# Where the block sums of a seven-product phase are made: four instructions per unit on VectorE or on GpSimd

## The chip, the cores and the metric

The kernel runs on one core of one Trainium2 chip. The metric is the device time of one launch in microseconds (us); smaller is better. Three runs of the kernel before took 1160.32, 1160.54 and 1163.41 us, median 1160.54.

## The reference

One layer of a diffusion backbone over 512 latent and 256 context tokens with 1024 channels. The part that matters here is the second feed-forward block, which works on the 512 latent tokens alone:

```python
def swiglu(h, w1, w3, w2):
    return (jax.nn.silu(h @ w1) * (h @ w3)) @ w2

def ffn_sublayer(h_in, shift, scale, gate, norm_w, w1, w3, w2):
    h = modulate(rms_norm(h_in, norm_w), shift, scale)
    return h_in + 0.5 * gate * swiglu(h, w1, w3, w2)
...
x = ffn_sublayer(x, mx[6], mx[7], mx[8], norm3_w, ffn2_w1, ffn2_w3, ffn2_w2)
```

The inner width is 2816, which is 22 slices of 128. One slice, with its 128 columns of `w1` and of `w3`, is called a unit below.

## The kernel before

**Split products.** Every float32 matrix product is made of three products. Each operand is split into a high part (`oph`, rounded by ScalarE's copy) and a low part (`opl`, the remainder, a subtraction on VectorE), and `mm3` adds high x high, low x high and high x low. So each 128x512 piece of weights costs one ScalarE cast of 128x512 and, behind it, one VectorE subtraction of 128x512 (`Stream.operand`, `Stream.split`, L138 to L147).

**Seven products in place of eight.** Units 4 to 21 of this block (class `Winograd`, made at L1692, run at L1728) multiply a 2x2 grid of weight blocks by a 2x2 grid of token blocks with seven block products. On the weight side a unit's four blocks q0 to q3, which arrive together in one 1 MB load (tile `block`, 128x2048), give seven operands: q0, s = q2+q3, q1, q0' = s-q0, q2' = q0-q2, q3 and q1' = q1-q0'. The four sums are the subject of the change. They overwrite the block in place, except s, which has a tile of its own. In the kernel before, GpSimd makes them, apart from unit 4, whose sums VectorE makes.

**Order on TensorE.** A unit runs T1, B21, T2, T3, then B11 of the next unit, then T4 and B22 of its own (method `unit`, L750): seven products of 12 matmuls of 256 columns. Two of them, T4 and B22, add to PSUM banks that T3 and T1 filled. VectorE has to read those banks first (`ev_u3`: u3 = W+u2, then u3 = Z+u3, with W the bank of T3 and Z the bank of T1).

**Slots.** `Flow.slot` (L105) is called ahead of each product. It writes out, in this order, the first part of the evacuation of the product before, then one more operand from the list, then the rest of the evacuation. At most five operands (`OPS`) are alive, so an operand is written out about four products ahead of its use. In slot order VectorE's part of a unit is: u2 and operand s of the next unit; the two adds of u3 and operand q1; operand q0'; W+u2 and W*silu, operand q2', the low part gl of the result; Z+u2, operand q0 of the unit after, Z*u3 and gl; operand q3; operand q1'.

**What sets the order.** The whole phase stands under `nc.ordered = "all"` (L1727): every instruction of VectorE, ScalarE, GpSimd and TensorE keeps the order in which it is written (`Pinned`, L60, is why nearly all rows of the profile carry the line L60). Each engine works off its queue in that order.

**Between the units.** After units 4, 8, 12, 16 and 18 a part of the down projection runs (`down_flow`, L638), with four slices each, two after unit 18: eight column blocks of 12 (6) matmuls of 512 columns, one operand of `w2` (from tiles `raw`) for each 4 matrix tiles, and one update of `x` by VectorE per column block. The last part (units 18 to 21) is written without pinned order, and a scheduler placed its first column blocks ahead of T4 of unit 21.

Of the kernel before, what the change touches and what calls it, by code (L numbers as in the profile page):

```python
# [173 lines left out]
def layer_kernel(ctx: ExitStack, tc: tile.TileContext, xT, wfirst, wst, wada, wuq, wkpe, cols, wrope, vnw, rope, out):  # L174
    nc = Core(tc)
# [6 lines left out]
    st = Stream(nc, raws, opp, OPS, wst)  # L182
# [81 lines left out]
    u0, rw0 = st.raw_pool.tile([P, 2048], F32, tag="block", bufs=BLOCKS, name="block_first"), st.raw()  # L264
# [137 lines left out]
    class SsqAcc:  # L402
        def __init__(self, pool, n, eng):
            self.pool, self.n, self.eng = pool, n, eng
            self.acc = None
            self.squares = []
# [259 lines left out]
    U_UP2 = U_IN + 22  # L666
# [11 lines left out]
    class Winograd:  # L678


        def __init__(self, pool, n, u0, blocks, g_tile, sl_bufs):
            self.sl_bufs = sl_bufs
            self.ready = (None,)
            self.pool, self.n, self.u0, self.blocks, self.g_tile = pool, n, u0, blocks, g_tile

# [10 lines left out]
        def wants(self, f):  # L696
            q, s1, eng = [], [], []

            def first():
                if self.ready[0] != f:  # L700
                    self.prep(f)
                q[:], s1[:], eng[:] = self.ready[1], [self.ready[2]], [self.ready[3]]
                a = st.operand(q[0])
                eng[0].tensor_sub(q[2], q[0], q[2])
                eng[0].tensor_sub(q[0], s1[0], q[0])
                return a

            def third():
                a = st.operand(q[1])
                eng[0].tensor_sub(q[1], q[1], q[0])  # L710
                return a

            of = lambda i: lambda: st.operand(q[i])
            return first, lambda: st.operand(s1[0]), third, of(0), of(2), of(3), of(1)

        def plan(self, flow, f0, downs, late=False):
# [132 lines left out]
    blocks = {"B11": hb(0, 0), "B21": hb(4, 0), "B22": hb(4, 384), "T1": hb(0, 384)}  # L849
# [65 lines left out]
    wino = Winograd(gp, 384, U_UP1, blocks, g_tile, 1)  # L915
# [698 lines left out]
    f2 = f2ctx.enter_context(tc.tile_pool(name="ffn2", bufs=2))  # L1614
# [74 lines left out]
    evac(0, 1)  # L1689
    diffs(3)  # L1690
    blocks = {"B11": B11, "B21": B21, "B22": B22, "T1": T1, "T2": T2, "T3": T3, "T4": T4}
    wino = Winograd(f2, 256, U_UP2, blocks, g2_tile, 2)  # L1692
    wino.prep(NPLAIN2, nc.vector)
    flow = Flow(OPS)
    wino.plan(flow, NPLAIN2, lambda f: [(CHUNKS2[ci], U_DN2 + starts2[ci]) for ci in ends2(f)])
# [141 lines left out]
```

## Time and profile before

| What | Value |
|---|---|
| Median of three runs | 1160.54 us |
| Span of the profiled execution | 1160.9 us |
| TensorE busy | 1139.5 us, 98% |
| VectorE busy | 906.1 us, 78% |
| ScalarE busy | 532.0 us, 46% |
| GpSimd busy | 320.9 us, 28% |
| Mean granted TensorE clock | 0.999 |
| The changed phase (units 4 to 21) | about 850 to 1141 us of the span |

A row of the timeline reads: start in us, duration in us, engine, line, operation, tile written <- tiles read, shapes, how many were merged; in brackets how long the engine sat idle before it and what ended that. Buffer numbers are left out of names, and `u2`, `u3`, `p1` and `s1` appear as `u`, `u`, `p` and `s`. A chain row reads: start, duration, engine, tile and line. A group row reads: line, engine, operation, tiles, shapes, count, then busy time, mean ns of one and idle time before them. VectorE's rows overlap a little: a 128x512 subtraction is listed with 0.68 us, and an independent instruction behind it starts 0.60 us after it did. One profiled execution gives all these rows.

### The profile page before, as it was taken

The numbers are of one execution on the slowest core, as the hardware profiler recorded it, in microseconds if no ns is written. First come the engines' busy times: TensorE is split into PE (matmuls) and PEld (weight loads), VectorE is DVE, ScalarE is ACT, GpSimd is POOL, SyncE is SP. The second block draws the span as 40 slices with busy tenths as digits, with TensorE's granted clock in tenths as the row PEclk, the third lists the DMA queues.
The fourth block names the chain that finished last, engine by engine and source line by source line (L and its number), as shares of the span: only waits on it lengthen the run. The fifth ranks groups of instructions, "written<-read, shape, count | busy, mean of one in ns | idle before, by whom it ended". The sixth has DMA issues, their size and how long they took to land. (4 is left out here: it accounts for less than half of the span.)

```text
span 1160.9 us, 18702 instructions
## 1 busy us (share of the span) xinstructions
PE 1139.5 (98%) x7070; PEld 1071.9 (92%) x7070; DVE 906.1 (78%) x1668; ACT 532.0 (46%) x1075; POOL 320.9 (28%) x279
## 2 busy tenths in 40 slices
PE   9999999999999999999999999999999999999998
PEld 5699999999999999999988788999999989898997
DVE  4778799889888779866746969869876959686884
ACT  4455431441244213444745549876543535353441
POOL 0011401320333013300017637670013325142330
PEclk9999999999999999999999999999999999999999
DMA  9441244334334664412242111002221322333312
GB/s 351 146 140 37 91 145 137 119 127 164 110 127 145 210 209 158 144 57 82 82 144 90 57 37 55 19 1 76 72 92 55 132 87 74 109 110 109 110 37 91
DMA packets 34650, 125.89 MB, mean 108 GB/s; under 512 B 3584, under 2 KB 10496, under 8 KB 29056
## 3 DMA queue, kind: packets, MB, share of 16 engines
q1 hardware_dynamic: 34416, 124.63, 31.3%
q8 instruction: 56, 0.92, 0.3%
q14 instruction: 34, 0.28, 0.1%
q10 hardware_dynamic: 144, 0.06, 0.0%
HBM read 122.58 MB, written 2.10 MB: 107 GB/s over the span
## 5 line engine op out<-in xcount | busy, mean ns | idle before, releaser
L60 DVE TENSOR_TENSOR opl<-block,oph 128x512 fp32r<-128x512 f32 x216 | 190.6, 888 | 35.5 <-ACT oph L60 33.4
L60 POOL TENSOR_TENSOR block<-block 128x512 f32<-128x512 f32 x70 | 103.7, 1481 | 393.5 <-DVE opl L60 390.8
L60 ACT CAST oph<-block 128x512 fp32r<-128x512 f32 x216 | 134.0, 621 | 144.6 <-PE mm L60 91.7
L60 PE MATMUL mm<-gh,oph 128*128 128x384 f32 (+1 forms) x440 | 155.2, 353 | 0.0
L60 PE MATMUL mm<-gl,oph 128*128 128x384 f32 (+1 forms) x440 | 154.9, 352 | 0.0
L60 PE MATMUL mm<-gh,opl 128*128 128x384 f32 (+1 forms) x440 | 154.9, 352 | 0.0
L60 DVE SCALAR_TENSOR_TENSOR x<-mm,g,x 128x256 f32<-128x256 f32 (+2 forms) x184 | 83.0, 490 | 49.9 <-PE mm L60 49.3
L60 ACT CAST oph<-raw 128x512 fp32r<-128x512 f32 x106 | 64.4, 619 | 93.8 <-PE mm L60 68.0
L60 PEld LDWEIGHTS mm<-gh,opl 128*128 128x128 f32 x440 | 82.6, 188 | 5.7
L60 PEld LDWEIGHTS mm<-gh,oph 128*128 128x128 f32 x440 | 82.6, 188 | 5.6
L60 PEld LDWEIGHTS mm<-gl,oph 128*128 128x128 f32 x440 | 82.6, 188 | 5.5
L60 DVE TENSOR_TENSOR opl<-raw,oph 128x512 fp32r<-128x512 f32 x106 | 73.2, 704 | 9.5 <-ACT oph L60 9.0
L60 POOL TENSOR_TENSOR s<-block 128x512 f32<-128x512 f32 x35 | 52.3, 1495 | 101.8 <-DVE gl L60 73.3
L60 POOL TENSOR_TENSOR block<-s,block 128x512 f32<-128x512 f32 x35 | 47.5, 1357 | 77.0 <-DVE opl L60 76.6
L60 PE MATMUL mm<-hl,oph 128*128 128x384 f32 x192 | 64.6, 336 | 1.8 <-DVE hl L60 1.8
L60 PE MATMUL mm<-hh,oph 128*128 128x384 f32 x192 | 64.5, 336 | 0.0
L60 PE MATMUL mm<-hh,opl 128*128 128x384 f32 x192 | 64.3, 335 | 0.0
L60 DVE SCALAR_TENSOR_TENSOR junk<-raw,cb 128x1024 bf16<-128x1024 f32 x48 | 60.3, 1263 | 0.1
L60 PE MATMUL one<-hh,oph 128*128 128x384 f32 x144 | 48.7, 338 | 0.0
L60 PE MATMUL one<-hl,oph 128*128 128x384 f32 x144 | 48.7, 338 | 0.0
L60 PE MATMUL one<-hh,opl 128*128 128x384 f32 x144 | 48.6, 337 | 0.0
L60 DVE SCALAR_TENSOR_TENSOR raw<-raw,cb 128x1024 f32<-128x1024 f32 x32 | 41.0, 1289 | 7.7 <-DMA raw<-wada 7.4
(649 smaller groups left out, 3461.6 us busy)
## 6 DMA issues: line engine op xcount, KB each, us to landing
raw<-wst SPq DMA_DIRECT2D x77, 512.0 KB, 3.7
block<-wst SPq DMA_DIRECT2D x36, 1024.0 KB, 4.9
raw<-wada SPq DMA_DIRECT2D x56, 512.0 KB, 4.0
block<-wada SPq DMA_DIRECT2D x7, 1024.0 KB, 7.4
x<-xT SPq DMA_DIRECT2D x6, 512.0 KB, 6.7
raw<-wfirst SPq DMA_DIRECT2D x8, 256.0 KB, 6.4
out<-x SPq DMA_DIRECT2D x7, 256.0 KB, 2.2
block_first<-wada SPq DMA_DIRECT2D x2, 512.0 KB, 8.0
```

The costliest lines, as they stand in the source:

```text
L60: return lambda *a, **k: self.tc.keep_in_program_order(f(*a, **k))
```

## The change

For this phase alone (`on_vector=True`) the four sums of each unit from 5 on are made by VectorE, each in the slot of an operand. The TensorE, ScalarE and DMA instructions stay the same, and so does the list of operands. Unit 4 keeps VectorE and gets the new places too. The first feed-forward block's seven-product phase keeps GpSimd.

```diff
-        def __init__(self, pool, n, u0, blocks, g_tile, sl_bufs):
-            self.sl_bufs = sl_bufs
+        def __init__(self, pool, n, u0, blocks, g_tile, sl_bufs, on_vector=False):
+            self.sl_bufs, self.on_vector = sl_bufs, on_vector
...
             of = lambda i: lambda: st.operand(q[i])
+            v = nc.vector
+
+            def first_v():
+                if self.ready[0] == f:
+                    q[:], s1[:] = self.ready[1], [self.ready[2]]
+                else:
+                    r = st.block(wst, (self.u0 + 2 * f) // 2)
+                    q[:] = [r[:, i * 512 : i * 512 + 512] for i in range(4)]
+                return st.operand(q[0])
+
+            def sum_v():
+                if not s1:
+                    s1.append(self.tmp("s1", 512, 2))
+                    v.tensor_add(s1[0], q[2], q[3])
+                return st.operand(s1[0])
+
+            def third_v():
+                v.tensor_sub(q[2], q[0], q[2])
+                return st.operand(q[1])
+
+            def second_v():
+                v.tensor_sub(q[0], s1[0], q[0])
+                return st.operand(q[0])
+
+            def fourth_v():
+                v.tensor_sub(q[1], q[1], q[0])
+                return st.operand(q[1])
+
+            if self.on_vector:
+                return first_v, sum_v, third_v, second_v, of(2), of(3), fourth_v
             return first, lambda: st.operand(s1[0]), third, of(0), of(2), of(3), of(1)
...
-    wino = Winograd(f2, 256, U_UP2, blocks, g2_tile, 2)
+    wino = Winograd(f2, 256, U_UP2, blocks, g2_tile, 2, True)
```

`nc.vector` is the pinned engine here, so a sum stands in VectorE's queue directly ahead of the low-part subtraction of the operand with which it is written. `st.operand` first writes ScalarE's cast of the operand, then VectorE's subtraction that reads both.

## The prediction

> **What bounds the kernel now.** I read the page first, for the engine that is never idle, then the chain of waits for this phase, then the timelines of VectorE, TensorE, GpSimd and ScalarE over one unit.
>
> ```profile
> span 1160.9 us, 18702 instructions
> PE 1139.5 (98%) x7070; PEld 1071.9 (92%) x7070; DVE 906.1 (78%) x1668; ACT 532.0 (46%) x1075; POOL 320.9 (28%) x279
> ```
>
> TensorE sets the time. The chain of waits runs over it:
>
> ```profile
> 894.87 5.76 PE mm L60 x48
> 900.63 1.44 PE one L60 x12
> 902.07 2.91 PE mm L60 x24
> ```
>
> These rows give a unit's length: four products 5.76, the next unit's B11 1.44, T4 and B22 2.88, together 10.08 us, with no gap between products. The gaps that there are stand ahead of T4:
>
> ```profile
> 911.89 0.28 PE L60 MATMUL mm<-b11h,opl 128*128 128x256 f32 x1
> 913.19 0.36 PE L60 MATMUL one<-t4h,oph 128*128 128x256 f32 x1 [1.02 <-ACT oph L60]
> ...
> 923.68 0.36 PE L60 MATMUL mm<-t4h,oph 128*128 128x256 f32 x1 [0.19 <-DVE u L60]
> ```
>
> ```profile
> L60 PE MATMUL mm<-t4h,oph 128*128 128x256 f32 x36 | 10.7, 298 | 0.6 <-DVE u L60 0.4
> L60 PE MATMUL one<-t4h,oph 128*128 128x256 f32 x36 | 10.4, 289 | 2.3 <-ACT oph L60 2.1 <-DVE u L60 0.2
> ```
>
> The last two rows are groups over the time from unit 4 on and hold T4's matmuls of high parts, the first of each product among them: 2.9 us idle. Matmuls follow each other every 0.12 us, though one is listed with 0.28, so counted from start to start a gap is 0.16 longer (911.89 to 913.19 is 1.30, less 0.12: 1.18). Eight such gaps make 2.9 + 8 x 0.16 = 4.2 us. That is all that this phase can give back.
>
> Why T4 waits is seen on VectorE, here from one u3 to the next:
>
> ```profile
> 901.30 0.88 DVE L60 TENSOR_TENSOR u<-mm,u 128x256 f32<-128x256 f32 x2
> 902.09 0.68 DVE L60 TENSOR_TENSOR opl<-block,oph 128x512 fp32r<-128x512 f32 x1
> 903.03 1.73 DVE L60 TENSOR_TENSOR opl<-block,oph 128x512 fp32r<-128x512 f32 x1 [0.25 <-ACT oph L60]
> 904.68 0.42 DVE L60 TENSOR_TENSOR mm<-mm,u 128x256 f32<-128x256 f32 x1
> 905.14 0.43 DVE L60 TENSOR_TENSOR mm<-mm,sl 128x256 f32<-128x256 f32 x1
> 905.48 1.80 DVE L60 TENSOR_TENSOR opl<-block,oph 128x512 fp32r<-128x512 f32 x1
> 907.21 0.41 DVE L60 TENSOR_TENSOR gl<-mm,gh 128x256 fp32r<-128x256 f32 x1
> 907.54 0.42 DVE L60 TENSOR_TENSOR mm<-mm,u 128x256 f32<-128x256 f32 x1
> 907.87 1.12 DVE L60 TENSOR_TENSOR opl<-block,oph 128x512 fp32r<-128x512 f32 x1
> 908.92 0.42 DVE L60 TENSOR_TENSOR mm<-mm,u 128x256 f32<-128x256 f32 x1
> 909.77 0.43 DVE L60 TENSOR_TENSOR gl<-mm,gh 128x256 fp32r<-128x256 f32 x1 [0.44 <-ACT gh L60]
> 910.30 1.49 DVE L60 TENSOR_TENSOR opl<-block,oph 128x512 fp32r<-128x512 f32 x2
> 911.70 0.42 DVE L60 TENSOR_TENSOR u<-one,p 128x256 f32<-128x256 f32 x1
> 912.03 0.68 DVE L60 TENSOR_TENSOR opl<-s,oph 128x512 fp32r<-128x512 f32 x1
> 912.63 0.88 DVE L60 TENSOR_TENSOR u<-one,u 128x256 f32<-128x256 f32 x2
> ```
>
> This cycle takes 912.63 - 901.30 = 11.33 us, longer than TensorE's 10.08. The first add of u3 ends at 912.63 + 0.42 = 913.05 and T4, which adds to the bank it reads, starts at 913.19: 0.14 later. (The profile names a cast, but that cast's tile was long split; the gap at 923.68 names `u`.) So T4 starts 0.14 us after u3's first add, and where VectorE's cycle exceeds 10.08 us the difference appears ahead of T4.
>
> **The change part by part.**
>
> *Removed: GpSimd's sums, and with them VectorE's slow subtractions.*
>
> ```profile
> 905.44 1.30 POOL L60 TENSOR_TENSOR s<-block 128x512 f32<-128x512 f32 x1 [1.23 <-DMA block<-wst]
> ```
>
> ```profile
> L60 DVE TENSOR_TENSOR opl<-block,oph 128x512 fp32r<-128x512 f32 x98 | 92.7, 953 | 13.3 <-ACT oph L60 11.5
> L60 DVE TENSOR_TENSOR opl<-raw,oph 128x512 fp32r<-128x512 f32 x28 | 18.9, 681 | 0.1
> L60 DVE TENSOR_TENSOR opl<-s,oph 128x512 fp32r<-128x512 f32 x16 | 11.0, 685 | 0.3
> ```
>
> The same subtraction means 0.95 us from `block` and 0.68 from `raw` or `s`. The slow ones run beside a GpSimd sum: that of 905.48 starts 0.04 after GpSimd's of 905.44 and lasts 1.80. With all seven at 0.60 spacing the cycle is: u3 0.80, operands q1 and q0' 1.20, W twice 0.80, operand 0.60, gl and Z+u2 0.66, operand 0.60, Z*u3 to gl 0.85 (908.92 to 909.77), gl to the next operand 0.53, that and q1' 1.20, u2 0.33, operand s 0.60: 8.2 us. So the removal returns 11.3 - 8.2 = 3.1 us of VectorE a unit.
>
> The Trainium skill ("SBUF — State Buffer", section "SBUF: two separate sides") says that VectorE and GpSimd share a port pair under an exclusive lock, and that the loser blocks for the whole instruction. By it the subtraction of 905.48 would wait to 906.74 and end near 907.4; the row ends at 907.28, so the trace agrees. By that rule too the sum has seven fast subtractions.
>
> *Added: four sums a unit.* VectorE makes such a sum in 0.69 us when GpSimd is quiet (unit 4 has one):
>
> ```profile
> 850.15 0.69 DVE L60 TENSOR_TENSOR block<-block 128x512 f32<-128x512 f32 x1
> ```
>
> Four at 0.60 spacing: +2.4 us, cycle 10.6.
>
> *Added: a wait behind three of them.* Where GpSimd made the sum, the cast of s, q0' or q1' could run while VectorE did other things. Now VectorE's queue holds sum, then the subtraction of that very operand, which needs ScalarE's cast, which needs the sum. Nothing may pass: u3, and T4 behind it, queue there. The price by rows:
>
> ```profile
> 909.37 0.37 ACT L60 CAST gh<-mm 128x256 fp32r<-128x256 f32 x1 [1.01 <-DVE mm L60]
> 909.64 0.63 ACT L60 CAST oph<-block 128x512 fp32r<-128x512 f32 x1
> ```
>
> VectorE's row of 908.92 ends at 909.34, ScalarE's cast starts at 909.37 and ends at 909.74, VectorE goes on at 909.77: 0.03 each way, and a 128x512 cast is 0.63. From a sum's start to the subtraction's start: 0.69 + 0.03 + 0.63 + 0.03 = 1.39 in place of 0.60, +0.79 each, three times: +2.4. q2' escapes, since q1's and q0's operands lie between its sum and its use. Bounds: nothing (casts somehow early), cycle 10.6; or the waits in full with the subtractions still at 0.95, 13.0 + 7 x 0.27 = 14.9. I take 13.0 (8.2 + 2.4 + 2.4): the fast rows are those without GpSimd beside them, and GpSimd has nothing left here.
>
> *From the cycle to the time.* Per unit T4 is late by 13.0 - 10.08 = 2.9 us more, wherever a full cycle lies between two T4s:
> - 7 full cycles (to units 6, 7, 10, 11, 14, 15, 20): 7 x 2.9 = 20.3.
> - 4 cycles to a unit ahead of a down part (8, 12, 16, 18): s gives way to a `raw` operand without a sum, so 1.39 less, 11.6: 4 x 1.5 = 6.0.
> - 6 first units (4, 5, 9, 13, 17, 19), where VectorE has caught up:
>
> ```profile
> 884.63 0.28 PE L60 MATMUL one<-t1h,oph 128*128 128x256 f32 x1
> ```
>
> ```profile
> 886.15 0.62 ACT L60 CAST oph<-block 128x512 fp32r<-128x512 f32 x1 [0.92 <-PE one L60]
> ```
>
> Unit 5: the cast of q3 waits for T1's end, 886.15, so q3's subtraction starts at 886.80, the sum q1' at 887.40, its subtraction at 888.79, u2 at 889.39, the sum s at 889.72, its subtraction at 891.11, u3 at 891.71, ending at 892.13; T4 can go at 892.27 where 884.63 + 5 x 1.44 = 891.83 was due: 0.45, say 0.5 each: 3.0. (If u2 alone waited, 0.1.)
> - The end: TensorE fills the time ahead of unit 21's T4 with the last down part:
>
> ```profile
> 1138.51 0.43 DVE L60 TENSOR_TENSOR one<-one,u 128x256 f32<-128x256 f32 x1 [3.96 <-PE one L60]
> ```
>
> VectorE waits 3.96 us there, so that T4 costs nothing; the filler's first `raw` subtraction comes behind unit 20's late queue, about 0.8.
>
> Inside the down parts I cost the sums at nothing: a column block lasts 2.72 us (next rows), and update 0.67, sum to subtraction 1.39 and subtraction 0.60 make 2.66. That cover is nearly used up.
>
> ```profile
> 876.67 0.75 DVE L60 SCALAR_TENSOR_TENSOR x<-mm,g,x 128x512 f32<-128x512 f32 x1 [1.37 <-PE mm L60]
> ...
> 879.39 0.75 DVE L60 SCALAR_TENSOR_TENSOR x<-mm,g,x 128x512 f32<-128x512 f32 x1 [1.37 <-PE mm L60]
> ```
>
> ```profile
> block<-wst SPq DMA_DIRECT2D x36, 1024.0 KB, 4.9
> ```
>
> The block loads neither move nor multiply. A buffer comes free with the subtraction of q1'; the first cast from its new load is due 9.0 us of VectorE's queue later (0.60, u2 0.33, s 1.99, u3 0.80, q2' and q1 1.20, q0' 1.99, W 0.80, operand 0.60, gl and Z+u2 0.66), and landing takes 4.9, so I cost it at nothing too.
>
> Sum: 20.3 + 6.0 + 3.0 + 0.8 = 30.1 us of gaps in place of 4.2: +25.9, so 1160.9 + 25.9 = 1186.8 for the span; the median run stands 0.4 below the profiled one: 1186.4.
>
> **The rivals.**
> - *Only throughput counts.* If the casts did not hold VectorE, the cycle would be 10.6. A first unit would then leave some 0.6 us of slack ahead of T4, and a full cycle uses 0.5 of it: about 1.5 us of gaps in all, 1158 us, and 1156.3 with none. For it: 3.1 us of contention go and only 2.4 come. Against it: the queue's written order. It decides from a cycle below about 11.0, where gaps would again sum to some 4 us. The Trainium skill ("GPSIMD Engine Reference", section "Engine selection") recommends VectorE for elementwise work on a tile, GpSimd being about twice as slow for two inputs; the rows (0.69 against 1.30) agree, and this rival is what that rule would give. Chance 0.08.
> - *The waits are shorter or partly covered.* With one full wait of three the cycle is 11.4, with two 12.2: at 11.8 the full cycles cost 7 x 1.7 and the others some 3: 1160.5 + 15 - 4.2 = 1171. For it: the second subtraction of 910.30 shows no wait for its cast. Against: that cast hung on no VectorE sum just ahead. Chance 0.11.
> - *More than the sum.* Subtractions stay at 0.95, or VectorE is still late when a down part or a load needs it: at 14.9, 7 x 4.8 + 4 x 3.4 + 4 = 51, so 1160.5 + 51 - 4.2 = 1207. For it: the thin cover of 0.06 us. Against: the `raw` and `s` rows. Chance 0.07.
> - *The change does not do what it says:* sums that move away from their operands. The phase's order is pinned; 0.01, time unchanged.
>
> **How the numbers follow.** My forecast has 0.73; its time is 1186.5, its own range 1180 to 1193 (a tenth of a us on the cycle is worth 1.1 us over eleven cycles; I allow 0.6). The range to record reaches into the second and third rivals: 1172 to 1198. About 0.3% (3.5 us) can be told from no change. Faster: half of the first rival, 0.04. Same: the rest of it and the last, 0.05. Slower: 0.91.
>
> **What would show it.** VectorE's u3 to u3 cycle of a middle unit near 13.0 us; three idle stretches of about 0.7 us on VectorE a unit, ended by the cast, ahead of subtractions from `s` and `block`; subtractions from `block` near 0.69; gaps near 2.9 us ahead of T4 in units 6, 7, 10, 11, 14, 15, 20 and near 1.5 in 8, 12, 16, 18; down parts without gaps; GpSimd idle after 846 us. A cycle under 11 us, or sums whose subtractions follow after 0.60, would prove me wrong.

## The result, and the profile after

The changed kernel takes 1192.6 us (median of 5 runs, 1191.6 to 1194.8), the kernel before 1160.5 (5 runs, 1159.7 to 1163.4). The ratio is 1.0268, with a 95% interval of 1.0254 to 1.0283: 32.1 us slower, where 26.0 were forecast. Five runs more of the changed kernel, beside twenty of the kernel before, gave 1.0262 (1.0248 to 1.0276).

First the page of the changed kernel: the span, then each engine's busy time and share.

```profile
span 1189.7 us, 18651 instructions
PE 1144.9 (96%) x7070; PEld 1074.9 (90%) x7070; DVE 918.0 (77%) x1736; ACT 531.6 (45%) x1075; POOL 225.7 (19%) x211
```

GpSimd has 68 instructions fewer and VectorE 68 more (17 units of four sums). VectorE is busy only 11.9 us longer, and still the span grows by 28.8: most of what was added is not work, it is waiting. Where that shows is in TensorE's groups of T4's high-part matmuls (count, then busy time, mean ns, and idle time ahead with what ended it):

```profile
L60 PE MATMUL mm<-t4h,oph 128*128 128x256 f32 x36 | 11.6, 323 | 16.6 <-DVE u L60 11.2 <-ACT oph L60 5.4
L60 PE MATMUL one<-t4h,oph 128*128 128x256 f32 x36 | 10.8, 299 | 8.4 <-DVE u L60 6.5 <-ACT p L60 1.9
```

2.9 us of idle time ahead of T4 have become 25.0. TensorE's timeline has it unit by unit; these are the first matmuls of T4 of units 5, 6, 7 and 8:

```profile
893.49 0.35 PE L60 MATMUL one<-t4h,oph 128*128 128x256 f32 x1 [0.47 <-ACT p L60]
...
906.59 0.36 PE L60 MATMUL mm<-t4h,oph 128*128 128x256 f32 x1 [2.80 <-DVE u L60]
...
919.70 0.36 PE L60 MATMUL one<-t4h,oph 128*128 128x256 f32 x1 [2.81 <-DVE u L60]
...
931.35 0.36 PE L60 MATMUL mm<-t4h,oph 128*128 128x256 f32 x1 [1.35 <-ACT oph L60]
```

From T4 to T4 it is 13.10 and 13.11 us in full cycles and 11.65 ahead of a down part, against 10.08 of TensorE's own work. VectorE's timeline over the same unit, from one u3 to the next, has the reason:

```profile
906.03 0.88 DVE L60 TENSOR_TENSOR u<-mm,u 128x256 f32<-128x256 f32 x2
906.82 0.68 DVE L60 TENSOR_TENSOR block<-block 128x512 f32<-128x512 f32 x1
907.42 0.68 DVE L60 TENSOR_TENSOR opl<-block,oph 128x512 fp32r<-128x512 f32 x1
908.02 0.68 DVE L60 TENSOR_TENSOR block<-s,block 128x512 f32<-128x512 f32 x1
909.45 0.69 DVE L60 TENSOR_TENSOR opl<-block,oph 128x512 fp32r<-128x512 f32 x1 [0.74 <-ACT oph L60]
...
914.71 0.69 DVE L60 TENSOR_TENSOR block<-block 128x512 f32<-128x512 f32 x1
916.14 0.69 DVE L60 TENSOR_TENSOR opl<-block,oph 128x512 fp32r<-128x512 f32 x1 [0.74 <-ACT oph L60]
...
917.08 0.68 DVE L60 TENSOR_TENSOR s<-block 128x512 f32<-128x512 f32 x1
918.53 0.69 DVE L60 TENSOR_TENSOR opl<-s,oph 128x512 fp32r<-128x512 f32 x1 [0.76 <-ACT oph L60]
919.13 0.88 DVE L60 TENSOR_TENSOR u<-one,u 128x256 f32<-128x256 f32 x2
```

The cycle is 919.13 - 906.03 = 13.10 us. Three times a sum is followed by 0.74 or 0.76 us of nothing and then by the subtraction of what it summed (908.02 to 909.45, 914.71 to 916.14, 917.08 to 918.53). The sum q2' at 906.82 has no such wait: its subtraction comes two operands later. The chain of waits walks the same loop; here is the wait behind 908.02, one row for each link (start, duration, engine, tile):

```profile
908.02 0.69 DVE block L60
908.80 0.63 ACT oph L60
909.45 0.69 DVE opl L60
```

From the sum's end to the cast 0.09 us, the cast 0.63, 0.02 back. In the groups of VectorE the subtractions from `block` have become as fast as the others, 0.687 in place of 0.953, and the waits stand ahead of these and of those from `s`:

```profile
L60 DVE TENSOR_TENSOR opl<-block,oph 128x512 fp32r<-128x512 f32 x98 | 67.2, 687 | 28.3 <-ACT oph L60 27.3
L60 DVE TENSOR_TENSOR opl<-s,oph 128x512 fp32r<-128x512 f32 x16 | 11.1, 691 | 12.2 <-ACT oph L60 12.2
```

### The profile page after: what moved, and what is told of

Its sections match the earlier page's. It is cut to its first block, busy times and chain, and to the rows that moved or that the text cites. A ratio compares the mean times of both kernels' runs of the same rounds, so it can differ in the third digit from the quotient of the medians.

```text
span 1189.7 us, 18651 instructions
## 1 busy us (share of the span) xinstructions
PE 1144.9 (96%) x7070; PEld 1074.9 (90%) x7070; DVE 918.0 (77%) x1736; ACT 531.6 (45%) x1075; POOL 225.7 (19%) x211
## 5 line engine op out<-in xcount | busy, mean ns | idle before, releaser
L60 DVE TENSOR_TENSOR opl<-block,oph 128x512 fp32r<-128x512 f32 x216 | 164.2, 763 | 50.1 <-ACT oph L60 48.7
L60 POOL TENSOR_TENSOR block<-block 128x512 f32<-128x512 f32 x36 | 53.2, 1478 | 250.1 <-DVE opl L60 248.7
L60 ACT CAST oph<-s 128x512 fp32r<-128x512 f32 x36 | 22.3, 620 | 64.5 <-DVE s L60 29.1
L60 POOL TENSOR_TENSOR s<-block 128x512 f32<-128x512 f32 x18 | 29.8, 1657 | 91.1 <-DVE gl L60 73.2
```

Of the source, the lines that this page charges most:

```text
L60: return lambda *a, **k: self.tc.keep_in_program_order(f(*a, **k))
```

## The experiments

The open question was not whether VectorE waits, but whether these waits are the whole loss. Rivals: the sums' own time on VectorE, the new places of the sums, or TensorE's granted clock, which falls in the changed kernel (below). Where a kernel below keeps the sums on VectorE, it changes where in the queue they stand. All ratios are to the kernel before on the same chip.

**No sum directly ahead of its cast.** All four sums stay on VectorE, each behind some operand that was loaded or summed earlier, so that its own operand comes a slot or more later:

```diff
-                return st.operand(q[0])
+                a = st.operand(q[0])
+                self.early = q, s1
+                if s1:
+                    early()
+                else:
                     s1.append(self.tmp("s1", 512, 2))
                     v.tensor_add(s1[0], q[2], q[3])
...
+                return a
...
+            def q3_v():
+                a = st.operand(q[3])
+                early()
+                return a
...
-                return first_v, sum_v, third_v, second_v, of(2), of(3), fourth_v
+                return first_v, lambda: st.operand(s1[0]), of(1), of(0), q2_v, q3_v, of(1)
```

`early` makes q2' and q0' of the next unit; `q2_v` writes operand q2' and then the sum q1'.

> All 68 sums stay on VectorE, but each is made one or more slots ahead of the operand that reads it: s in the slot of q0, q2' and q0' in the slot of the q3 before, q1' in the slot of q2'. Theory (a cast's wait behind a sum holds VectorE's queue): the u3-to-u3 cycle falls from 13.1 to about 10.6 us, the gaps ahead of T4 from 29.5 us to at most 3, and the time to 1158 us (1156 to 1161). Rival (four more VectorE instructions a unit are what costs, wherever they stand): the cycle stays near 13 us and the time within 3 us of 1192.

Measured: 1169.5 us, ratio 1.0066 (1.0052 to 1.0080). With the same 68 sums on the same engine, 2.0 of the 2.7 per cent are gone. But 1158 was not reached. VectorE's timeline of this kernel:

```profile
903.39 0.88 DVE L60 TENSOR_TENSOR u<-mm,u 128x256 f32<-128x256 f32 x2
...
905.66 0.43 DVE L60 TENSOR_TENSOR mm<-mm,u 128x256 f32<-128x256 f32 x1 [0.20 <-PE mm L60]
...
911.53 0.69 DVE L60 TENSOR_TENSOR block<-block 128x512 f32<-128x512 f32 x1
912.25 0.69 DVE L60 TENSOR_TENSOR block<-s,block 128x512 f32<-128x512 f32 x1
...
914.39 0.87 DVE L60 TENSOR_TENSOR u<-one,u 128x256 f32<-128x256 f32 x2
```

The cycle is 11.00 us, not 10.6. Two small pieces explain most of it: the add of W waits 0.20 for TensorE (this is T4's own lateness coming round: u3 releases T4, T4's end releases W), and a sum that reads the result of the sum ahead of it starts 0.72 after it, not 0.60. What that makes ahead of T4 stands in the view of T4's tile (idle us, times):

```profile
  DVE u L60: 8.1, 11
```

Eleven gaps, 8.1 + 11 x 0.16 = 9.9 us, about 0.9 behind every full cycle and every cycle ahead of a down part. At a cycle of 11.0 the prediction's first rival had some 4 us of gaps, since it gave each first unit 0.6 us of slack; there is none, the second unit already waits in full. T4's gaps are 5.7 us more than the 4.2 of before, the time 7.8 us more; in the profiled runs 0.9 us of the rest lie ahead of this phase, and what else there is stays open.

**One wait less, one wait more.** In the first of these kernels s is summed a slot earlier, behind operand q0; two waits are left. In the second q0' goes to a tile of its own, and q2' is summed directly ahead of its own cast; that makes four.

```diff
-                return st.operand(q[0])
-
-            def sum_v():
+                a = st.operand(q[0])
                 if not s1:
                     s1.append(self.tmp("s1", 512, 2))
                     v.tensor_add(s1[0], q[2], q[3])
+                return a
+
+            def sum_v():
                 return st.operand(s1[0])
```

```diff
-                v.tensor_sub(q[2], q[0], q[2])
...
-                v.tensor_sub(q[0], s1[0], q[0])
+                q0 = q[0]
+                q[0] = self.tmp("d0", 512, 2)
+                v.tensor_sub(q[0], s1[0], q0)
+                s1[0] = q0
...
+            def q2_v():
+                v.tensor_sub(q[2], s1[0], q[2])
+                return st.operand(q[2])
...
-                return first_v, sum_v, third_v, second_v, of(2), of(3), fourth_v
+                return first_v, sum_v, third_v, second_v, q2_v, of(3), fourth_v
```

> As the changed kernel, but s alone is made early, in the slot of q0; q0' and q1' still stand directly ahead of their operands. Theory: one wait of 0.79 us less in a full cycle, 12.3 us in place of 13.1 (7 x 0.8 = 5.5 us less), the first units lose their gap of 0.6 (3 us less), and the cycles ahead of a down part take in the s of the next unit (4 x 0.6 = 2.4 us more): about 6 us less, 1186 us. Rival (the load of the sums): 1192 us, cycle 13.1.

> As the changed kernel, but the fourth sum, q2', is moved directly ahead of its operand too (q0' goes to a tile of its own so that q0 lives on). The count of VectorE instructions is the same. Theory: one more wait of 0.79 us in every cycle, full ones 13.9 us and those ahead of a down part 12.4: 11 x 0.8 = 8.7 us more than the changed kernel, about 1201 us. Rival (the load of the sums): 1192 us as before.

Measured: 1183.3 us with two, ratio 1.0183 (1.0166 to 1.0200); 1211.7 with four, ratio 1.0429 (1.0408 to 1.0451), and 1208.9, ratio 1.0410 (1.0388 to 1.0433), when it ran again. T4 of units 6 and 7 with two waits, then of units 5, 6 and 7 with four:

```profile
905.37 0.36 PE L60 MATMUL mm<-t4h,oph 128*128 128x256 f32 x1 [1.35 <-DVE u L60]
...
917.62 0.35 PE L60 MATMUL one<-t4h,oph 128*128 128x256 f32 x1 [1.94 <-DVE u L60]
```

```profile
897.76 0.36 PE L60 MATMUL one<-t4h,oph 128*128 128x256 f32 x1 [0.47 <-ACT p L60]
...
911.71 0.36 PE L60 MATMUL mm<-t4h,oph 128*128 128x256 f32 x1 [3.65 <-DVE u L60]
...
925.67 0.35 PE L60 MATMUL one<-t4h,oph 128*128 128x256 f32 x1 [2.16 <-DVE u L60]
```

The cycle is 12.25, 13.10 and 13.95 us for two, three and four waits: 0.85 us each, evenly. From none to two it was 1.25, since the kernel with none has the small idle pieces named above. Whether it is s or q2' that is added makes no difference to the cycle; the number of waits does. The time does not grow as evenly: 9.3 us from two to three (1183.3 to 1192.6), then 16 to 19. With two waits the cycle is as expected and the time 2.7 us under the expected 1186: in the second unit behind a down part T4 waits 1.35 us (unit 6) and not the 1.94 of the next (unit 7), 0.6 less in each of units 6, 10, 14 and 20. With four the cycle is as expected and the time 8 to 11 us over the expected 1201. What else four waits cost is taken up below.

**The same places on GpSimd.** The changed kernel's order with the sums back on GpSimd: `v = nc.vector if self.ready[0] == f else nc.gpsimd`.

> The places of the changed kernel in the written order, but units 5 to 21 make the four sums on GpSimd. Theory (VectorE's own queue is what waits): GpSimd's queue runs ahead of VectorE's as it did, so the time is that of the kernel before, 1160 us within 3, with subtractions from block at a mean near 0.95 us. Rival (spreading the sums over four slots is what costs, on whichever engine): above 1180 us.

Measured: 1164.3 us, beside 1161.8 for the kernel before, ratio 1.0017 (1.0006 to 1.0028). The group of subtractions:

```profile
L60 DVE TENSOR_TENSOR opl<-block,oph 128x512 fp32r<-128x512 f32 x98 | 91.7, 942 | 13.1 <-ACT oph L60 11.4
```

Their idle time is 13.1 as before the change (13.3), and they are slow again. So it is not the spreading over four slots that costs; the same order with another engine as summer has no such waits. Most of the 2 us above the kernel before is unit 4, whose sums VectorE still makes in the new places: its B21 waits 0.70 us there and its T4 0.34.

**No sums at all.** This is an edit of the kernel before: the sums of units 5 to 21 are left out, and the operands are split from the blocks as they were loaded; all else runs.

```diff
+            def bare():
+                r = st.block(wst, (self.u0 + 2 * f) // 2)
+                q[:] = [r[:, i * 512 : i * 512 + 512] for i in range(4)]
+                return st.operand(q[0])
+
             of = lambda i: lambda: st.operand(q[i])
+            if self.bare and self.ready[0] != f:
+                return bare, of(2), of(1), of(0), of(2), of(3), of(1)
```

> The kernel before without the four sums of units 5 to 21: the seven operands are split from the blocks as they were loaded, so their count, casts and subtractions stay, and the products are of other operands. Theory (GpSimd's sums slow VectorE's subtractions, nothing else makes the gaps): subtractions from block at 0.69 us in this phase, no gap ahead of T4 above 0.2 us, 3 to 4 us under the kernel before, 1157 us. Rival (the subtractions from block are slow of themselves): mean near 0.95 us, gaps and time as before.

Measured: 1159.3 us, ratio 0.9972 (0.9963 to 0.9981), and no gap ahead of T4. The difference is the 3 to 4 us that were expected; 1157 was expected from 1160.5, and beside it here the kernel before took 1162.7.

```profile
L60 DVE TENSOR_TENSOR opl<-block,oph 128x512 fp32r<-128x512 f32 x114 | 78.4, 687 | 25.6 <-ACT oph L60 23.9
```

(The idle time in this row holds up nobody: T4 never waits.) Without GpSimd's sums beside it the subtraction takes 0.687 us, so these were what slowed it to 0.953. The Trainium skill ("SBUF — State Buffer", section "SBUF: two separate sides") gives the exclusive lock that the prediction drew on as the mechanism; this run agrees with it. And 3.4 us (1162.7 to 1159.3) is all that the sums cost in the kernel before.

**TensorE kept busy.** In the changed kernel the granted clock means 0.990 to 0.996 over its runs, in the kernel before 0.997 to 1.000. To see whether this costs time, 20 matmuls that nobody reads were put into the idle time ahead of T4 in the seven units after a full cycle:

```diff
+                if f in warm:
+                    w = self.blocks["T4"][0]
+                    for i in range(20):
+                        nc.tensor.matmul(nxt[0][1][:, 256:512], w[:, 0, :128], w[:, 0, :], start=True, stop=True, skip_group_check=True)
```

> The changed kernel with 20 more matmuls of 256 columns (2.4 us), whose results nobody reads, behind B11 in units 6, 7, 10, 11, 14, 15 and 20, where TensorE stood idle 2.9 us. Theory A (the idle stretches lower the granted clock, and that costs time of its own): the clock stays at 1.00 and the time falls by 1 to 3 us against the changed kernel on the same chip. Theory B (VectorE's cycle hides the slower matmuls): the clock stays at 1.00 and the time is the same within 1 us. Neither changes the spacing of T4, 13.1 us in middle units.

The changed kernel ran beside it once more:

> The changed kernel as it is, beside the others on the same chip: 1.027 times the kernel before, clock between 0.990 and 0.996, with slower runs where the mean clock is lower.

Measured: 1193.0 us, ratio 1.0264 (1.0250 to 1.0278), beside 1192.7 and 1.0262 without the matmuls. The clock stood at 0.999 to 1.000. T4 of unit 6 now waits 0.41 us behind the extra matmuls in place of 2.80, and starts no earlier in its cycle:

```profile
905.13 2.56 PE L60 MATMUL one<-t4h 128*128 128x256 f32 x20
...
908.10 0.35 PE L60 MATMUL mm<-t4h,oph 128*128 128x256 f32 x1 [0.41 <-DVE u L60]
```

The lower clock costs the changed kernel nothing that can be measured: VectorE sets the pace there, and TensorE's slower matmuls use up idle time that it would have had in the next unit. In the profiled run of the changed kernel T4 of unit 10 ran slowly (shown at the end); the idle time ahead of T4 of unit 11 is 1.52 us for that, in place of 2.81 in unit 7, and from T4 to T4 it is 13.10 us all the same.

The same with four waits, 28 such matmuls ahead of a full cycle's T4 and 16 ahead of a down part, beside the kernel with four waits again:

> e5_four_waits with extra matmuls whose results nobody reads behind B11: 28 (3.4 us) in units 6, 7, 10, 11, 14, 15, 20 and 16 (1.9 us) in 8, 12, 16, 18. T4 to T4 stays 13.9 us in middle units. Theory A (in e5 the clock fell in units ahead of a down part, where TensorE and not VectorE sets the time, so slower matmuls cost in full): the clock rises from 0.983 to above 0.995 and the time falls towards the 1201 us that the waits alone give, at least 5 us below e5. Theory B (the slower matmuls are hidden in e5 as they are in the changed kernel): the clock rises, the time stays within 2 us of e5.

> e5_four_waits as it is, beside it on the same chip: 1.043 times the kernel before, clock near 0.984.

Measured: 1206.3 us, ratio 1.0374 (1.0359 to 1.0389), against 1.0410 (1.0388 to 1.0433) without: 2.6 us less, at a clock of 0.997 to 0.999 in place of 0.983 to 0.987. The intervals just touch, and the gain lies between the two theories, the 5 us of A and the 2 us of B. The traces show where the lower clock costs: in a T4 ahead of a down part, behind which TensorE sets the pace. Here are T4 of unit 12 and of unit 13, with the down part between them, in the kernel with four waits:

```profile
1011.28 0.46 PE L60 MATMUL mm<-t4h,oph 128*128 128x256 f32 x1 [2.21 <-ACT oph L60]
...
1045.33 0.35 PE L60 MATMUL one<-t4h,oph 128*128 128x256 f32 x1 [0.47 <-ACT p L60]
```

From one to the other it is 34.05 us. In the changed kernel's profiled run, and in this kernel's with the extra matmuls, it is 32.55 or 32.56. Units 16 to 17 took 34.04 as well, so this profiled run lost 3.0 us there. Unit 4's matmuls were slow too, behind the 2.21 us that its B21 waited, and cost 1.4 us; no extra matmuls stand there. So the slow matmuls cost some 4.4 us in this run, of the 8 to 11 over the expectation, and the extra matmuls can give back 3.0 of it. Two first units add 2.4 us more: the gap in unit 4 grew from 0.9 to 2.4 us and that of unit 19 from 1.0 to 1.9. From T4 of unit 20 to the last matmul it is 1.5 us longer than in the changed kernel, and the time ahead of the phase, which no edit touches, differs by 1.4 us either way between the runs; the causes of these two stay open.

**Sums in VectorE's idle moments.** The unit has 0.44 us ahead of the second gl, where VectorE waits for ScalarE's copy gh. Here s stands there, q2' ahead of q3's subtraction and q0' behind it, q1' behind the operand q0':

```diff
-                g_split(Z, gh[:, n:], gl[:, n:])
+                nc.scalar.copy(gh[:, n:], Z)
+                self.ahead(2)
+                nc.vector.tensor_sub(gl[:, n:], Z, gh[:, n:].bitcast(F32))
...
+            def q3_v():
+                self.ahead(1)
+                a = st.operand(q[3])
+                self.ahead(0)
+                return a
```

`ahead(left)` writes the next of the three sums s, q2', q0' until `left` are to come.

> All sums on VectorE, made ahead of their operands as in e1_early_sums, and placed where that run's VectorE still stood idle: s between the product Z*u3 and the low part gl that waits for its cast, q2' ahead of q3's subtraction, q0' behind it, q1' between u3 and W+u2, where T4's end is waited for. Theory (VectorE's cycle against TensorE's 10.08 us sets the gaps): the cycle would be 9.9 us of work, so it falls to TensorE's 10.08, the gaps to at most 1.5 us in all, and the time to 1158 us, 2 to 4 us under the kernel before on the same chip. Rival (the load of the sums costs wherever VectorE makes them): no better than e1_early_sums, 0.6% above the kernel before.

Measured: 1161.0 us (11 runs), beside 1162.7 for the kernel before (20 runs): ratio 0.9990 (0.9982 to 0.9999). VectorE's timeline:

```profile
903.40 0.89 DVE L60 TENSOR_TENSOR u<-mm,u 128x256 f32<-128x256 f32 x2
...
909.21 0.69 DVE L60 TENSOR_TENSOR s<-block 128x512 f32<-128x512 f32 x1
909.81 0.42 DVE L60 TENSOR_TENSOR gl<-mm,gh 128x256 fp32r<-128x256 f32 x1
910.14 0.69 DVE L60 TENSOR_TENSOR block<-block 128x512 f32<-128x512 f32 x1
910.74 0.69 DVE L60 TENSOR_TENSOR opl<-block,oph 128x512 fp32r<-128x512 f32 x1
911.34 0.69 DVE L60 TENSOR_TENSOR block<-s,block 128x512 f32<-128x512 f32 x1
...
913.47 0.89 DVE L60 TENSOR_TENSOR u<-one,u 128x256 f32<-128x256 f32 x2
```

In these rows sums and subtractions follow each other every 0.60 us with no idle time, s fills the hole ahead of gl, and no sum reads the one directly ahead of it. The cycle is 10.07 us, and TensorE's 10.08 sets the pace: from T4 to T4 it is 10.14 to 10.18 us, and no gap ahead of T4 is left that the profile lists. So the change's aim, GpSimd's sums on VectorE, costs nothing in these places. It is the fastest kernel here that makes the sums, 1.8 us under the kernel before, where 2 to 4 were expected, of the 3.4 that were to be had; but that is 0.1%, with an interval that ends just below 1, and no more than the no change of the prediction's terms.

## Why the prediction was right, and what was off

- *GpSimd's silence speeds up the subtractions.* Right: 0.687, as costed, and shown by the kernel without sums.
- *Three waits of 0.79 us.* Right in number, place and mechanism, as the kernels with none, two and four such waits show; 1.43 to 1.45 us from a sum to its subtraction where 1.39 was worked out. The hop to ScalarE was taken as 0.03, and the chain has 0.09 behind a sum of 128x512.
- *Full cycles 13.0, ahead of a down part 11.6.* 13.10 and 11.65. Seven times 3.02 is 21.1 (20.3 forecast), four times 1.57 is 6.3 (6.0).
- *First units, 0.5 each.* Too small. In 5, 9, 13 and 17 T4 waits 0.47 us, start to start 0.63. Unit 19 has more, and unit 4 a gap in a place that the prediction didn't look at: B21, which waits for ScalarE's copy p of the bank that it fills; that copy stood behind the cast of q0', and this cast now waits for VectorE's sum. First ScalarE's rows there, then TensorE's of units 4, 19 and the last down part:

```profile
853.68 1.14 ACT L60 CAST oph<-block 128x512 fp32r<-128x512 f32 x2 [1.09 <-DVE block L60]
854.72 0.36 ACT L60 COPY p<-mm 128x256 f32<-128x256 f32 x1
```

```profile
855.14 0.39 PE L60 MATMUL mm<-b21h,oph 128*128 128x256 f32 x1 [0.69 <-ACT p L60]
...
1138.70 0.36 PE L60 MATMUL one<-t4h,oph 128*128 128x256 f32 x1 [0.87 <-DVE u L60]
...
1161.39 0.50 PE L168 MATMUL mm<-gh,oph 128*128 128x512 f32 x1 [0.72 <-ACT oph L139]
```

  With 0.16 added to each idle time: 0.85 + 4 x 0.63 + 1.03 = 4.4 where 3.0 stood. The end, 0.72 + 0.16 = 0.9, was forecast with 0.8.
- *Down parts cost nothing.* Right, by as little as was said: sum, wait and subtraction fit exactly between two updates of `x`, and the second update starts without any idle time:

```profile
875.65 0.68 DVE L60 TENSOR_TENSOR s<-block 128x512 f32<-128x512 f32 x1
877.10 0.69 DVE L60 TENSOR_TENSOR opl<-s,oph 128x512 fp32r<-128x512 f32 x1 [0.76 <-ACT oph L60]
877.71 0.75 DVE L60 SCALAR_TENSOR_TENSOR x<-mm,g,x 128x512 f32<-128x512 f32 x1
```

- *The sum.* 21.1 + 6.3 + 4.4 + 0.9 = 32.7 us in place of 4.2, +28.5; the span grew by 28.8. The mis-sized terms are the first units (1.4) and the cycle's tenth of a us (1.1).
- *From the span to the time.* This step was faulty: "the median run stands 0.4 below the profiled one" compared a run's time with a span. In every run the time is 1.7 to 2.1 us above its span (1191.62 beside 1189.7 in the profiled one of the changed kernel), so the span of 1160.9 belonged to a run of about 1162.7, some 2 us slower than the median one. Of the 6.1 us between 1186.5 and 1192.6, 2.9 are the span's growth beyond 25.9, 1.9 are the time around the span that was not added, 0.4 was wrongly taken off, and 0.9 is that the median run's span (1190.6) is above the profiled one's. All four go the same way, so no luck made the forecast better than its terms. Why the profiled run of the kernel before was slower than the median one is not known.
- *The rivals.* "The waits are shorter or partly covered" didn't happen: all three waits stand in full. "Only throughput counts" describes the kernel with sums in idle moments: the rule behind it is sound for the work, and what failed in the changed kernel is the order. "More than the sum" didn't happen: neither slow subtractions nor late down parts.

## What to carry to other kernels

On an engine that works off its queue in order, an instruction's price is its duration plus the time until the next one in the queue may run: a sum directly ahead of something that needs another engine's answer to it cost 0.69 + 0.75 us here, and a sum placed a slot or more ahead of its operand cost 0.60. So before moving work to an engine with time to spare, list what stands behind each moved instruction, and place producers ahead of independent work, or where the engine waits for something else anyway. And when a forecast is summed on a span, add what lies around the span before comparing it with a time.

## What was not expected of the hardware

TensorE's granted clock falls behind some of the idle stretches. Windows of the changed kernel: length, then busy us (and count) of the five engines, the granted clock, the DMA share and GB/s.

```profile
972.00:978.00 6.00, 3.20 (x24) 3.03 (x22) 4.46 (x10) 2.03 (x4) 0.00 (x0) 0.87 0.45 160
978.00:984.00 6.00, 6.00 (x45) 6.00 (x45) 4.79 (x11) 2.88 (x7) 0.00 (x0) 0.84 0.04 15
```

TensorE's rows behind that idle stretch (T4 of unit 10):

```profile
977.00 0.55 PE L60 MATMUL mm<-t4h,oph 128*128 128x256 f32 x1 [2.80 <-DVE u L60]
977.35 0.42 PE L60 MATMUL mm<-t4l,oph 128*128 128x256 f32 x1
```

Here T4's matmuls follow each other every 0.21 us in place of 0.12, after 2.80 us of idle time. From 977 to 979 us the granted clock is 0.50; from 980 on it is 1.00. After the same 2.80 us in unit 6 (906.59 above) they kept to 0.12, at 1.00. The Trainium skill ("TensorE: Matmul & The Clock Gate", section "What's actually happening") says that the clock is halved after an idle window of about 3.4 us, and that these windows run freely; the trace agrees with the halving and with its depending on more than the length of the gap, but 2.80 us were enough here, and 2.21 in unit 12 of the kernel with four waits (1011.28 above). The kernels with extra matmuls showed that this costs nothing measurable while another engine sets the pace, and some 3 us, in one comparison, where the slow matmuls stand ahead of a down part.
